# A fp32 trunk on one core: seven products for chunk 7 of a fast group, later transposes, and alternating first groups

## The chip, the core and the metric

The kernel runs on one core of a Trainium2 chip. The engines are TensorE (PE in the profile, with its weight loads as PEld), VectorE (DVE), ScalarE (ACT), GpSimd (POOL) and SyncE (SP), which issues most DMAs. The metric is the device time of one execution in microseconds, as the median of several runs.

## The reference

Two decoder layers on x of 256 x 2048 in fp32. Layer 0 is a recurrent block (RG-LRU) and a SwiGLU FFN; then one K/V projection; layer 1 is sliding-window attention with sinks and a second SwiGLU FFN.

```python
def swiglu_ffn(x, g, w_in, w_out):
    h = rms_norm(x, g)
    gate, up = jnp.split(h @ w_in, 2, axis=-1)
    return x + (jax.nn.silu(gate) * up) @ w_out

def recurrent_block(x, g, w_in, conv_w, conv_b, w_rg, b_rg, w_ig, b_ig, lam, w_out):
    h = rms_norm(x, g)
    y_branch, x_branch = jnp.split(h @ w_in, 2, axis=-1)
    xb = causal_depthwise_conv(x_branch, conv_w, conv_b)
    hs = rg_lru(xb, w_rg, b_rg, w_ig, b_ig, lam)
    return x + (hs * jax.nn.gelu(y_branch)) @ w_out
...
    for layer in range(DEPTH):
        if layer < N_REC:
            x = recurrent_block(...)
        else:
            if layer == N_REC:
                k_band, v_band = shared_kv(x, kv_norm_g, w_kv, k_norm_g)
            x = attn_block(...)
        x = swiglu_ffn(x, norm2_g[layer], ffn_w_in[layer], ffn_w_out[layer])
```

D_MODEL is 2048 and D_FF 5632, so an FFN has w_in of 2048 x 11264 and w_out of 5632 x 2048.

## The kernel before

**Products in three parts.** Each fp32 operand is split in a high part (rounded to the format that the matmul reads) and a low part (the rest); a product is high x high + high x low + low x high. So a 128x128 block of weights costs three matmuls over 256 columns (the 256 tokens).

**Jobs.** The work is a list of 704 jobs, each with a weight tile of 512 KB (128 x 1024). `stream` (L381) goes through them: at job i it issues the load of job i+4 on SP into one of 4 raw tiles (`load`, L334), splits the weights of job i+3 into one of 4 pairs of hi and lo tiles (`split`, L351: ACT copies hi at L359, DVE subtracts lo at L360), and then issues the matmuls of job i. Other work (norms, gates, recombinations) is written as generators that are advanced between jobs by budgets of DVE and ACT time; a scheduler then orders the rows on each engine, so the order is to be read from the built program.

**Groups.** A group is 8 jobs (chunks, 0 to 7) over the 2048 input features that fill 4 banks of PSUM; two sets of 4 banks take turns. `group` (L411) issues 24 matmuls of 128x256 a chunk at L407. A chunk named in its `sync` has three pairs of them (both columns of a bank half) as one matmul of 128x512 instead, 21 instructions for the same work; the two banks that hold these need another copy and addition at the end.

**FFN.** w_in has 22 groups of 8 chunks, w_out 4 groups of 22 chunks. In w_in the groups 4, 6, ..., 20 are fast (`FAST`). In a fast group, the chunks named in `PAIRS` (0, 1, 2, 4, 5, 6) multiply 2x2 blocks by seven products (the Strassen-Winograd scheme) in place of eight: 21 matmuls at L565 in place of 24. They need combined activations, made once per FFN in `normed` (a tile mx[p] for every chunk of `PAIRS`; four operations on 128x128 blocks, a copy and a subtraction), and combined weights, made for each chunk in `mix` (L362): DVE adds and subtracts raw blocks (L371, L372, L373), ACT copies the high parts (L370 of the plain blocks, L374 of the combined ones), and DVE subtracts the low parts (L375, L376). Chunks 3 and 7 are plain, 24 matmuls at L565. In chunks 0 and 4 the products of combined weights come first, in the others last. At a fast group's end `joined` recombines the products on ACT and DVE, and appends four transposes on PE (L761, `turn`) to a list that `flush` empties: at chunk 4 of the next fast group, or for the last one at chunk `pre` of the end group, group 21. The groups between the fast ones, and the end group, are plain groups of 192 narrow matmuls each (L407); the end group has `sync` chunks 0, 3, 4 and 5. After it, `ffn_out` runs by `project`, whose chunks 0, 1, 2 have wide matmuls.

**LRU.** Its groups run in the order x0 x1 x2 g0 x3 g1 y0 ..., the first two being the first 16 jobs. The background task `first` (in `run`) prepares the 16 slices of x (a scaled copy on ACT, a subtraction on DVE, `gained`), then squares them for the norm (tiles sq), and the norm's matmuls (L516, L518) follow. x comes in four tiles of 512 KB; the first is loaded with job 0, the others by SP behind the loads of jobs 1, 2 and 3.

Of the kernel before, what the change touches and what calls it, by code (L numbers as in the profile page):

```python
# [21 lines left out]
ND = D // P  # L22
NH = DFF // P
# [26 lines left out]
class Trunk:  # L50
# [2 lines left out]

    ORDER = "x0 x1 x2 g0 x3 g1 y0 g2 g3 y1 g4 g5 y2 g6 g7 y3"
    NORM0 = 11
    NORM = 6
    MISC = 4

# [3 lines left out]
    SYNC = (0, 1, 2)  # L62
    PLAIN = 4
    FAST = tuple(range(4, 21, 2))
    PAIRS = (0, 1, 2, 4, 5, 6)
    EVEN = (0, 4)
    OWED = 9000.0
    BUSY = 780.0
# [7 lines left out]
    def __init__(self, ctx, tc, dram):  # L76
        self.tc, self.nc, self.d = tc, tc.nc, dram
        nc = self.nc
        const = ctx.enter_context(tc.tile_pool(name="const", bufs=1))
        psum = ctx.enter_context(tc.tile_pool(name="psum", bufs=1, space=bass.MemoryType.PSUM))  # L80
        self.par = const.tile([P, NPAR], F32, name="par")
        self.con = const.tile([P, NCON], F32, name="con")
        self.cc = const.tile([P, 32], F32, name="cc")
        self.rstd = [const.tile([P, T + 2], F32, name=f"rstd{i}") for i in range(2)]
        self.nm, self.nt = (const.tile([P, T + 2], F32, name=n) for n in ("nm", "nt"))
        self.r2 = const.tile([P, 2], F32, name="r2")
        self.rrs = [const.tile([P, 48], F32, name=f"rr{i}") for i in range(2)]
        self.zero = const.tile([P, P + T], F32R, name="zero")
        const.tile([P, PAD], F32, name="pad")
        self.raw = [const.tile([P, 1024], F32, name=f"raw{i}") for i in range(4)]  # L90
        self.hi = [const.tile([P, 1024], F32R, name=f"hi{i}") for i in range(4)]
        self.lo = [const.tile([P, 1024], F32R, name=f"lo{i}") for i in range(4)]
        self.tmps = deque(const.tile([P, T], F32, name=f"t{i}") for i in range(4))
        self.halves = deque(const.tile([P, T], F32, name=f"h{i}") for i in range(4))
        self.sq = deque(const.tile([P, T], F32, name=f"sq{i}") for i in range(3))
        self.acc = self.sq.popleft()
        self.whole = [deque((i, 0) for i in range(self.NEAR, self.WORK)), deque((i, 0) for i in range(self.NEAR))]
        self.stamp = 0
        self.tick = -2 * self.LD
        self.keep = False  # L100
        self.part = {(d, n): deque() for d in (F32, F32R) for n in (False, True)}
        self.spool = const
        for i in range(self.WORK):
            if i == self.NEAR:
                const.tile([P, 16], F32, name="step")
            const.tile([P, 4 * T], F32, tag=f"s{i}", name=f"s{i}")
        self.held = {}
        self.x, self.xt = [None] * 4, [None] * 4
        for i in range(4):
            self.place(i)  # L110
        self.dram = ctx.enter_context(tc.tile_pool(name="dram", bufs=1, space=bass.MemoryType.DRAM))
        self.away = {}
        self.sets = [[psum.tile([P, 512], F32, name=f"b{4 * i + j}") for j in range(4)] for i in range(2)]
        self.banks = deque(b for q in self.sets for b in q)
        self.misc = 0
        self.started = False
        self.jobs = []
        self.mixed = {}
        self.pend = deque()
        self.bg = deque()  # L120
        self.dve = 0.0
        self.act = 0.0
# [211 lines left out]
    def load(self, i):  # L334
        dma = self.nc.sync.dma_start
        raw, src = self.raw[i % 4], self.jobs[i][0]
        if i == 0:

            self.nc.scalar.dma_start(self.x[0][:, 0:2, :], self.d["x"][:, 0:2, :])
            self.nc.scalar.dma_start(self.par, self.d["par"])  # L340
            for h in range(2):
                dma(raw[:, 512 * h:512 * h + 512], src[:, 512 * h:512 * h + 512])
            dma(self.x[0][:, 2:4, :], self.d["x"][:, 2:4, :])
        else:
            dma(raw, src)
            if i < 4:
                dma(self.x[i], self.d["x"][:, 4 * i:4 * i + 4, :])
        if i == 4:
            dma(self.con, self.d["con"])

# [156 lines left out]

    def norm(self, r, wait=NORM):

# [48 lines left out]
    def fast_group(self, src, xn, mx, g, done, final):  # L558
# [49 lines left out]
        for c in range(8):  # L608
            def mm(hi, lo, c=c):
                if c == 0:  # L610
                    st["ps"] = self.bank4()
                if c == self.EVEN[1]:
                    self.flush()
                (fast if c in self.PAIRS else plain)(c, hi, lo)
                if c == 7:
                    done(st["ps"])
            self.jobs.append((src(c), mm, (c in self.PAIRS) + (c in self.EVEN)))

# [5 lines left out]
    def ffn(self, l, xs, r, gains, rn, col, out=None):  # L624
# [3 lines left out]
        xn = [Val() for _ in range(ND)]  # L628
# [64 lines left out]
        for g in range(NH // 2):  # L693
# [77 lines left out]
            src = lambda c, g=g: w[g, c]  # L771
            if g < self.PLAIN:
                self.group(src, ND, xs, start, g == self.PLAIN - 1, self.SYNC, four=True)
            elif g in self.FAST:
                self.fast_group(src, xn, mx, g, joined, g == self.FAST[-1])
            else:
                end = g == self.FAST[-1] + 1
                self.group(src, ND, xn, direct, g == NH // 2 - 1, (0, 3, 4, 5) if end else (), True, 3 if end else None)
            if g == 0:
                def begin():  # L780
                    self.spawn(normed())
# [4 lines left out]
        n = len(self.jobs)  # L786
# [57 lines left out]
    def lru(self, gains, rn):  # L844
# [149 lines left out]

        for step in self.ORDER.split():
            {"x": x_group, "y": y_group, "g": gates}[step[0]](int(step[1]))
        self.project(self.d["lru_out"], ND, zs, gains, rn)


# [307 lines left out]
    def run(self):  # L1307
        nc, d = self.nc, self.d
        self.rv = {i: Val() for i in range(4)}
        self.rstd = {0: self.rstd[0], 1: self.rstd[1], 2: self.rstd[0], 3: self.rstd[1]}  # L1310
        vals = lambda: [Val() for _ in range(ND)]
        self.xs0, x1, xk, x2, x3 = (vals() for _ in range(5))

        def first():
            for k in range(ND):
                self.gained(k, [(C_N1A, self.xs0)])
                yield 2 * (k == 1)
            for k in range(ND):
                yield from self.squares(k)
            yield from self.norm(0, self.NORM0)  # L1320
            self.decay()
        self.spawn(first())
        nc.vector.memset(self.zero[:, :].bitcast(F32), 0.0)
        p = self.bank()
        for _ in range(self.WARM):
            nc.tensor.matmul(p[:, 0:T], self.zero[:, 0:P], self.zero[:, P:P + T], start=True, stop=True)
        self.free_bank(p)

        self.lru([(C_N2A, x1)], 1)
        self.ffn(0, x1, 1, [(C_KVG, xk)], 2, C_N2A)  # L1330
        self.kv(xk, 2, [(C_N1B, x2)])
        self.attn(x2, 2, [(C_N2B, x3)], 3)
        self.ffn(1, x3, 3, None, None, C_N2B, d["out"])
        self.stream()
# [64 lines left out]
```

## Time and profile before

| | before |
|---|---|
| median of 3 runs | 1977.0 us (1976.61 to 1977.29) |
| the profiled execution | 1976.85 us, span 1975.1 us, clock 1.000 |
| PE busy | 1966.8 us, 16548 matmuls |
| DVE busy | 1514.6 us (77%) |
| ACT busy | 1131.8 us (57%) |
| L565, seven-product chunks and plain chunks of fast groups | 1224 + 1296 + 612 matmuls |
| DMA | 384.96 MB, mean 195 GB/s |

All rows are of one execution. "L407" is a line of the kernel; a row of a timeline is start, length, engine, line, operation, written tile, read tiles, and in brackets the idle time ahead with what ended it. A matmul's recorded length holds its way through the array; the distance from start to start is what it costs.

### The profile page before, as it was taken

Reading aid. Unit: us, or ns where it says so; the run is one execution under the profiler, and the core shown is the slowest. Engines: PE = TensorE matmul, PEld = TensorE weight load, DVE = VectorE, ACT = ScalarE, POOL = GpSimd, SP = SyncE. Lnnn points to the kernel's source line nnn. Section 1 sums busy time; section 2 is a strip of 40 time slices with the busy share of each in tenths; the row PEclk is TensorE's granted clock in tenths of the full one; section 3 lists DMA queues with packets and bytes.
Section 4 is the critical chain, followed back from the end, with each engine's and each line's share of the span. In section 5 each row is a group of like instructions: output and inputs, shape, how many; then the busy total and the mean of one; then the engine's idle time right before and its main releaser. Section 6 shows DMA issues by size and latency. Waiting matters only on the chain. (4 is left out here: it accounts for less than half of the span.)

```text
span 1975.1 us, 40195 instructions
## 1 busy us (share of the span) xinstructions
PE 1966.8 (100%) x16548; PEld 1925.4 (97%) x16548; DVE 1514.6 (77%) x2399; ACT 1131.8 (57%) x1656; POOL 0.2 (0%) x4
## 2 busy tenths in 40 slices
PE   9999999999999999999999999999999999999999
PEld 9999999999999999999998789999999999999999
DVE  8989868998888887554667776698889888954443
ACT  7788756555555566444556675565555555744442
POOL 0000000000000000000000000000000000000000
PEclk9999999999999999999999999999999999999999
DMA  7555665566555566556554335656555666666663
GB/s 272 191 191 178 216 217 192 186 206 208 202 199 197 200 218 224 194 190 201 194 182 145 122 118 171 213 186 206 191 199 200 203 207 202 235 203 203 203 204 128
DMA packets 107320, 384.96 MB, mean 195 GB/s; under 512 B 11904, under 2 KB 14080, under 8 KB 107136
## 3 DMA queue, kind: packets, MB, share of 16 engines
q1 hardware_dynamic: 106848, 381.99, 57.7%
q8 instruction: 129, 2.11, 0.4%
q14 instruction: 55, 0.45, 0.1%
q10 hardware_dynamic: 288, 0.40, 0.1%
HBM read 376.06 MB, written 6.29 MB: 194 GB/s over the span
## 5 line engine op out<-in xcount | busy, mean ns | idle before, releaser
L407 PE MATMUL b<-s,hi 128*128 128x256 f32 (+1 forms) x7934 | 1060.1, 281 | 1.6 <-ACT s L133 1.2
L407 PEld LDWEIGHTS b<-s,hi 128*128 128x128 f32 x7934 | 986.5, 188 | 14.7 <-ACT s L133 2.2
L360 DVE TENSOR_TENSOR lo<-raw,hi 128x1024 fp32r<-128x1024 f32 (+1 forms) x597 | 726.9, 1222 | 354.8 <-ACT hi L359 351.9
L359 ACT ACTIVATE hi<-raw 128x1024 fp32r<-128x1024 f32 (+1 forms) x597 | 628.3, 1056 | 502.3 <-PE b L407 400.9
L407 PE MATMUL b<-s,lo 128*128 128x256 f32 x4096 | 607.3, 277 | 0.0
L407 PEld LDWEIGHTS b<-s,lo 128*128 128x128 f32 x4096 | 530.4, 188 | 0.2
L374 ACT ACTIVATE s<-s 128x1024 fp32r<-128x1024 f32 x108 | 114.8, 1063 | 183.6 <-DVE s L373 183.6
L565 PE MATMUL b<-hi,s 128*128 128x256 f32 x1224 | 203.2, 277 | 0.0
L565 PEld LDWEIGHTS b<-hi,s 128*128 128x128 f32 x1224 | 174.1, 188 | 0.0
L565 PE MATMUL b<-s,s 128*128 128x256 f32 x1296 | 168.4, 279 | 0.0
L565 PEld LDWEIGHTS b<-s,s 128*128 128x128 f32 x1296 | 157.2, 189 | 0.0
L376 DVE TENSOR_TENSOR s<-s,s 128x1024 fp32r<-128x1024 f32 x108 | 132.0, 1223 | 23.6 <-ACT s L374 23.6
L565 PE MATMUL b<-lo,s 128*128 128x256 f32 x612 | 145.8, 277 | 0.0
L565 PEld LDWEIGHTS b<-lo,s 128*128 128x128 f32 x612 | 104.2, 188 | 0.0
L133 ACT ACTIVATE s<-s 128x512 fp32r<-128x512 f32 (+3 forms) x174 | 86.1, 523 | 30.4 <-DVE s L142 18.5
L370 ACT ACTIVATE hi<-raw 128x768 fp32r<-128x768 f32 x108 | 88.0, 839 | 24.2 <-issue 14.0
L375 DVE TENSOR_TENSOR lo<-raw,hi 128x768 fp32r<-128x768 f32 x108 | 101.5, 953 | 0.0
L371 DVE TENSOR_TENSOR s<-raw 128x512 f32<-128x512 f32 x108 | 74.3, 688 | 22.0 <-DMA raw<-in_ffn_in 21.6
L1289 PE MATMUL b<-hi,s 128*128 128x512 f32 x256 | 83.5, 407 | 0.0
L142 DVE TENSOR_TENSOR s<-s,s 128x512 fp32r<-128x512 f32 (+2 forms) x141 | 74.9, 559 | 4.7 <-ACT s L133 4.7
L133 ACT ACTIVATE s<-b 128x256 fp32r<-128x256 f32 (+4 forms) x134 | 58.8, 468 | 24.9 <-PE b L1263 6.8
L142 DVE TENSOR_TENSOR s<-b,s 128x512 f32<-128x512 f32 (+3 forms) x126 | 63.4, 533 | 5.3 <-ACT s L133 3.9
(115 smaller groups left out, 1101.0 us busy)
## 6 DMA issues: line engine op xcount, KB each, us to landing
raw<-in_ffn_in SPq DMA_DIRECT2D x352, 512.0 KB, 3.5
raw<-in_ffn_out SPq DMA_DIRECT2D x176, 512.0 KB, 3.4
raw<-in_lru_in SPq DMA_DIRECT2D x63, 512.0 KB, 3.8
raw<-in_lru_out SPq DMA_DIRECT2D x32, 512.0 KB, 4.1
raw<-in_w_q SPq DMA_DIRECT2D x32, 512.0 KB, 3.3
raw<-in_w_o SPq DMA_DIRECT2D x32, 512.0 KB, 3.5
raw<-in_gate SPq DMA_DIRECT2D x8, 512.0 KB, 3.9
away<-s SPq DMA_DIRECT2D x8, 512.0 KB, 3.6
```

Of the source, the lines that this page charges most:

```text
L133: self.nc.scalar.activation(out, in_, func, **kw)
L142: self.nc.vector.tensor_tensor(out, a, b, op)
L359: self.nc.scalar.activation(hi[:, q], raw[:, q], AF.Copy)
L360: self.nc.vector.tensor_tensor(lo[:, q], raw[:, q], hi[:, q].bitcast(F32), ALU.subtract)
L370: act(hi[:, q], raw[:, q], AF.Copy)
L371: tt(two(d[:, 0:2 * T]), two(raw[:, T:3 * T]), raw[:, 0:T].unsqueeze(1).to_broadcast([P, 2, T]), ALU.subtract)
L374: act(mh[:, :], d[:, :], AF.Copy)
L375: tt(lo[:, q], raw[:, q], hi[:, q].bitcast(F32), ALU.subtract)
L376: self.mark = tt(ml[:, :], d[:, :], mh[:, :].bitcast(F32), ALU.subtract)
L407: self.nc.tensor.matmul(ps[f][:, 0:c1 - c0], w, x2[k][:, c0:c1], start=f not in begun, stop=last and all(q[1] != f for q in todo[n + 1:]))
L565: nc.tensor.matmul(st["ps"][b][:, h % 2 * T:(h % 2 + n) * T], x, w, start=b not in st["begun"], stop=True, skip_group_check=True)
L1289: nc.tensor.matmul(st[g][b][:, :], x, q, start=c + kt == 0 and x is xh and q is wh, stop=c == 7 and kt == 1 and q is wl)
```

## The change

Three edits. Chunk 7 joins `PAIRS`, so that seven of eight chunks of a fast group go by seven products, and `normed` makes one more combined tile. The end group loses its wide matmuls, and its `flush` goes from chunk 3 to chunk 6. The first 16 jobs are put in another order: x0 and x1 alternate for six chunks (x0 c0, x1 c0, x0 c1, x1 c1, x0 c2, x1 c2), then the rest of x0 and the rest of x1; the x tiles 1, 2, 3 are loaded behind jobs 2, 5 and 7, and `first` waits until the tile it needs has been issued. Lines of the changed kernel are 2 to 4 higher up to L381, and 4 higher in the groups (L407 becomes L411, L565 L569, L761 L765, L376 L380).

```diff
--- before.py
+++ after.py
@@ -53,6 +53,7 @@
 
     ORDER = "x0 x1 x2 g0 x3 g1 y0 g2 g3 y1 g4 g5 y2 g6 g7 y3"
     NORM0 = 11
+    XLOAD = {2: 1, 5: 2, 7: 3}
     NORM = 6
     MISC = 4
 
@@ -62,7 +63,7 @@
     SYNC = (0, 1, 2)
     PLAIN = 4
     FAST = tuple(range(4, 21, 2))
-    PAIRS = (0, 1, 2, 4, 5, 6)
+    PAIRS = (0, 1, 2, 4, 5, 6, 7)
     EVEN = (0, 4)
     OWED = 9000.0
     BUSY = 780.0
@@ -110,6 +111,7 @@
             self.place(i)
         self.dram = ctx.enter_context(tc.tile_pool(name="dram", bufs=1, space=bass.MemoryType.DRAM))
         self.away = {}
+        self.got = 0
         self.sets = [[psum.tile([P, 512], F32, name=f"b{4 * i + j}") for j in range(4)] for i in range(2)]
         self.banks = deque(b for q in self.sets for b in q)
         self.misc = 0
@@ -343,8 +345,10 @@
             dma(self.x[0][:, 2:4, :], self.d["x"][:, 2:4, :])
         else:
             dma(raw, src)
-            if i < 4:
-                dma(self.x[i], self.d["x"][:, 4 * i:4 * i + 4, :])
+            if i in self.XLOAD:
+                n = self.XLOAD[i]
+                dma(self.x[n], self.d["x"][:, 4 * n:4 * n + 4, :])
+                self.got = n
         if i == 4:
             dma(self.con, self.d["con"])
 
@@ -775,7 +779,7 @@
                 self.fast_group(src, xn, mx, g, joined, g == self.FAST[-1])
             else:
                 end = g == self.FAST[-1] + 1
-                self.group(src, ND, xn, direct, g == NH // 2 - 1, (0, 3, 4, 5) if end else (), True, 3 if end else None)
+                self.group(src, ND, xn, direct, g == NH // 2 - 1, (), True, 6 if end else None)
             if g == 0:
                 def begin():
                     self.spawn(normed())
@@ -994,6 +998,8 @@
 
         for step in self.ORDER.split():
             {"x": x_group, "y": y_group, "g": gates}[step[0]](int(step[1]))
+        first = [8 * (i % 2) + i // 2 for i in range(6)]
+        self.jobs[:16] = [self.jobs[i] for i in first + [i for i in range(16) if i not in first]]
         self.project(self.d["lru_out"], ND, zs, gains, rn)
 
 
@@ -1313,6 +1319,8 @@
 
         def first():
             for k in range(ND):
+                while self.got < k // 4:
+                    yield 1
                 self.gained(k, [(C_N1A, self.xs0)])
                 yield 2 * (k == 1)
             for k in range(ND):
```

What stands on DVE where the last chunks of a fast group of FFN 0 are split, before (L371 to L376 are a mix, raw2 that of chunk 6; L360 is a plain split, the last two rows being chunk 7 and the next group's chunk 0):

```order
L376 TENSOR_TENSOR s2_5204<-s3_5202,s1_5203 128x1024
L375 TENSOR_TENSOR lo0_81<-raw0_73,hi0_77 128x768
L375 TENSOR_TENSOR lo1_82<-raw1_74,hi1_78 128x768
L371 TENSOR_TENSOR s5_5234<-raw2_75 128x512
L372 TENSOR_TENSOR s5_5234<-raw2_75,s5_5234 128x256
L375 TENSOR_TENSOR lo2_83<-raw2_75,hi2_79 128x768
L373 TENSOR_TENSOR s5_5234<-raw2_75,s5_5234 128x256
L376 TENSOR_TENSOR s3_5236<-s5_5234,s0_5235 128x1024
L360 TENSOR_TENSOR lo3_84<-raw3_76,hi3_80 128x1024
L360 TENSOR_TENSOR lo0_81<-raw0_73,hi0_77 128x1024
```

and now (lines 4 higher, raw2 chunk 6, raw3 chunk 7):

```order
L380 TENSOR_TENSOR s2_5216<-s5_5214,s4_5215 128x1024
L375 TENSOR_TENSOR s1_5246<-raw2_75 128x512
L379 TENSOR_TENSOR lo2_83<-raw2_75,hi2_79 128x768
L376 TENSOR_TENSOR s1_5246<-raw2_75,s1_5246 128x256
L375 TENSOR_TENSOR s3_5281<-raw3_76 128x512
L377 TENSOR_TENSOR s1_5246<-raw2_75,s1_5246 128x256
L376 TENSOR_TENSOR s3_5281<-raw3_76,s3_5281 128x256
L377 TENSOR_TENSOR s3_5281<-raw3_76,s3_5281 128x256
L380 TENSOR_TENSOR s5_5248<-s1_5246,s6_5247 128x1024
L379 TENSOR_TENSOR lo3_84<-raw3_76,hi3_80 128x768
L380 TENSOR_TENSOR s1_5283<-s3_5281,s0_5282 128x1024
L364 TENSOR_TENSOR lo0_81<-raw0_73,hi0_77 128x1024
```

The three additions of chunk 7 (on s3) now stand ahead of the last subtraction of chunk 6 (s5), and two subtractions of chunk 7 where one was.

On PE around the transposes of the last fast group in FFN 1's end group, before (hi3 and lo3 are the end group's chunk 3; b is a bank, s a tile of activations):

```order
L407 MATMUL b5_145<-s18_14431,lo2_83 128x256
L407 MATMUL b6_146<-s18_14431,lo2_83 128x256
L407 MATMUL b7_147<-s18_14431,lo2_83 128x256
L761 MATMUL b0_140<-con_62,s21_19098 128x128 x4
L407 MATMUL b6_146<-s9_14498,hi3_80 128x256
L407 MATMUL b4_144<-s9_14498,hi3_80 128x512 x2
L407 MATMUL b5_145<-s9_14498,hi3_80 128x512
L407 MATMUL b6_146<-s9_14498,hi3_80 128x256
```

and now:

```order
L411 MATMUL b5_145<-s19_14648,lo1_82 128x256
L411 MATMUL b6_146<-s19_14648,lo1_82 128x256
L411 MATMUL b7_147<-s19_14648,lo1_82 128x256
L765 MATMUL b0_140<-con_62,s27_19213 128x128 x4
L411 MATMUL b4_144<-s26_14747,hi2_79 128x256 x2
L411 MATMUL b5_145<-s26_14747,hi2_79 128x256 x2
L411 MATMUL b6_146<-s26_14747,hi2_79 128x256 x2
```

The transposes stand ahead of chunk 6 (hi2) instead of chunk 3, and the 128x512 matmuls behind them are gone.

SP's queue at the start, before (raw is a weight tile, s33 to s36 the tiles of x, con the constants):

```order
L342 DMA raw0_73<-in_lru_in 128x512 x2
L343 DMA s36_134<-in_x 128x512
L345 DMA raw1_74<-in_lru_in 128x1024
L347 DMA s35_135<-in_x 128x1024
L345 DMA raw2_75<-in_lru_in 128x1024
L347 DMA s34_136<-in_x 128x1024
L345 DMA raw3_76<-in_lru_in 128x1024
L347 DMA s33_137<-in_x 128x1024
L345 DMA raw0_73<-in_lru_in 128x1024
```

and now:

```order
L344 DMA raw0_73<-in_lru_in 128x512 x2
L345 DMA s36_134<-in_x 128x512
L347 DMA raw1_74<-in_lru_in 128x1024
L347 DMA raw2_75<-in_lru_in 128x1024
L350 DMA s35_135<-in_x 128x1024
L347 DMA raw3_76<-in_lru_in 128x1024
L347 DMA raw0_73<-in_lru_in 128x1024
L353 DMA con_62<-in_con 128x1026
L347 DMA raw1_74<-in_lru_in 128x1024
L350 DMA s34_136<-in_x 128x1024
```

The tiles s35, s34 and s33 moved behind the loads of jobs 2, 5 and 7.

## The prediction

> **What bounds the kernel now.** I read the page's busy rows first.
>
> ```profile
> span 1975.1 us, 40195 instructions
> PE 1966.8 (100%) x16548; PEld 1925.4 (97%) x16548; DVE 1514.6 (77%) x2399; ACT 1131.8 (57%) x1656; POOL 0.2 (0%) x4
> ```
>
> TensorE (PE) is busy for all but 8.3 us, so time can only come from fewer matmuls, a faster pace, or those 8.3 us. VectorE (DVE) is the next engine. The chain of waits says the same for the stretch the change touches, a pair of one fast and one plain group:
>
> ```profile
> 1395.25 9.96 PE b L565 x87
> 1405.20 0.44 PE b L761 x4
> 1405.64 9.96 PE b L565 x87
> 1415.60 21.76 PE b L407 x192
> ```
>
> 87 matmuls of a half fast group take 9.96 us (114.5 ns each); 192 of a plain group take 21.76 us (113.3 ns each). Nothing but PE stands in the chain there: DVE and ScalarE (ACT) keep ahead, and the question is whether they still do with the new work. The windows view gives the load in one such pair, among the heaviest on DVE:
>
> ```profile
> 1489.40:1531.50 42.10, 42.10 (x373) 42.10 (x372) 37.38 (x50) 23.15 (x28) 0.00 (x0) 1.00 0.60 208
> ```
>
> The columns are length, then PE, weight loads, DVE, ACT, POOL, granted clock, DMA share, GB/s. DVE has 4.7 us free of 42.1, ACT 19; the clock is full.
>
> **The change part by part.** *Chunk 7 by seven products.* The timeline of PE at the end of the last fast group shows a mixed chunk (6), a plain one (7), and the plain group behind them:
>
> ```profile
> 1705.10 0.39 PE L565 MATMUL b<-hi,s 128*128 128x256 f32 x2
> 1706.12 1.52 PE L565 MATMUL b<-s,s 128*128 128x256 f32 x12
> 1707.48 0.62 PE L565 MATMUL b<-hi,s 128*128 128x256 f32 x4
> 1710.20 1.98 PE L407 MATMUL b<-s,hi 128*128 128x512 f32 x13
> ```
>
> Chunk 6, 21 matmuls, runs from 1705.10 to 1707.48: 2.38 us. Chunk 7, 24 matmuls, runs to 1710.20: 2.72 us. The saving is 0.34 us a group, for 9 fast groups in each of 2 FFNs 18 x 0.34 = **-6.1 us** (the same as 54 matmuls x 113.3 ns). The end of a mixed chunk (twelve matmuls from mixed weights at 1706.12) does not slow what follows: the 24 behind it keep 113.3 ns.
>
> The Trainium skill ("TensorE: Matmul & The Clock Gate", section "Back-to-back issue gap") gives N/2.4 + 2.5 ns for an isolated warm matmul, 109.2 ns at 256 columns, and says that in a real stream of weight loads and matmuls both set the spacing. By the formula 54 matmuls would be an estimated 5.9 us; the row's 113.3 ns decides.
>
> What it costs elsewhere: chunk 7's weights are no longer split by one subtraction (L360) but mixed.
>
> ```profile
> L360 DVE TENSOR_TENSOR lo<-raw,hi 128x1024 fp32r<-128x1024 f32 x595 | 725.5, 1223 | 351.1 <-ACT hi L359 348.2
> L371 DVE TENSOR_TENSOR s<-raw 128x512 f32<-128x512 f32 x108 | 74.3, 688 | 22.0 <-DMA raw<-in_ffn_in 21.6
> L372 DVE TENSOR_TENSOR s<-raw,s 128x256 f32<-128x256 f32 x108 | 45.7, 423 | 2.3
> L373 DVE TENSOR_TENSOR s<-raw,s 128x256 f32<-128x256 f32 x108 | 45.7, 423 | 2.3
> L375 DVE TENSOR_TENSOR lo<-raw,hi 128x768 fp32r<-128x768 f32 x108 | 101.5, 953 | 0.0
> L376 DVE TENSOR_TENSOR s<-s,s 128x1024 fp32r<-128x1024 f32 x108 | 132.0, 1223 | 23.6 <-ACT s L374 23.6
> L374 ACT ACTIVATE s<-s 128x1024 fp32r<-128x1024 f32 x108 | 114.8, 1063 | 183.6 <-DVE s L373 183.6
> L370 ACT ACTIVATE hi<-raw 128x768 fp32r<-128x768 f32 x108 | 88.0, 839 | 24.2 <-issue 14.0 <-ACT hi L359 4.8 <-ACT hi L370 2.5
> ```
>
> On DVE 0.688 + 0.423 + 0.423 + 0.953 + 1.223 = 3.71 us in place of 1.22: 2.5 us more per fast group. The heaviest pair goes from 37.4 to at most 39.9 us of a new 41.8 (42.1 - 0.34): 95% busy, still under PE. ACT gets L370 and L374 (1.90 us) in place of one copy of about a microsecond, with 19 us free. Cost on the path nothing, as long as each mix is done in time, which is a matter of latency and not of load:
>
> ```profile
> 1701.04 1.22 DVE L376 TENSOR_TENSOR s<-s,s 128x1024 fp32r<-128x1024 f32 x1 [1.12 <-ACT s L374]
> 399.27 1.23 DVE L376 TENSOR_TENSOR s<-s,s 128x1024 fp32r<-128x1024 f32 x1 [0.46 <-ACT s L374]
> 400.42 4.62 DVE L360 TENSOR_TENSOR lo<-raw,hi 128x1024 fp32r<-128x1024 f32 x4
> 403.45 0.62 PE L565 MATMUL b<-hi,s 128*128 128x256 f32 x4
> ```
>
> In the steady state (first row) chunk 6's last mix ends at 1702.26 and is read from 1706.12 on: 3.9 us early. DVE waits 1.12 us for L374 just there, and in the new order the L371 to L373 of chunk 7 stand in that hole. Back to back, an instruction starts a little before the last one's recorded end (400.42 behind 399.27: 1.15 apart for 1.23), so L371 to L373 take some 1.3 us against 1.12; then L375 (0.87) and L376 (1.15). Chunk 7's mix ends at about 1704.5, and is read 1.02 us into the chunk (1706.12 - 1705.10), at 1708.50: **4 us early**; up to four short instructions of other work ahead of it leave 1.5 to 4.
>
> The first fast group of an FFN is tightest, for its mixes follow the catch-up on the norm. Its chunk 6 mix starts at 399.27 behind a hole of 0.46 only. The new three add 1.3 - 0.5 = 0.8 us, then 0.87 and two of 1.15: done at about 403.3, read at 403.45 + 1.02 = 404.47: about **1.1 us early**. I take 0; were the estimate wrong by more than that, the stall is the second rival's. The new tiles of the norm (four short operations of 128x128, a copy, a subtraction: below 2 us of DVE per FFN) fall into holes of the group before:
>
> ```profile
> 370.38 1.23 DVE L360 TENSOR_TENSOR lo<-raw,hi 128x1024 fp32r<-128x1024 f32 x1 [1.34 <-ACT hi L359]
> 373.08 0.69 DVE L371 TENSOR_TENSOR s<-raw 128x512 f32<-128x512 f32 x1 [1.47 <-DMA raw<-in_ffn_in]
> ```
>
> Those hold 2.8 us; if they did not cover it, it would come off the 1.1 us. No DMA is added in the FFNs and the weights' loads keep their order on SP's queue; they are gated by the buffers' release, which the shorter chunk makes earlier by 0.34 us.
>
> *The end group.* Its four chunks with wide matmuls become narrow ones. Ahead of the transposes and behind them stand:
>
> ```profile
> 1715.65 1.98 PE L407 MATMUL b<-s,hi 128*128 128x256 f32 x16
> 1717.46 1.07 PE L407 MATMUL b<-s,lo 128*128 128x256 f32 x8
> 1718.37 0.60 PE L761 MATMUL b<-con,s 128*128 128x128 f32 x4
> 1718.73 2.07 PE L407 MATMUL b<-s,hi 128*128 128x256 f32 x13
> 1720.63 1.07 PE L407 MATMUL b<-s,lo 128*128 128x256 f32 x8
> 1716.87 0.69 DVE L142 TENSOR_TENSOR s<-s 128x512 f32<-128x512 f32 x1
> ```
>
> Wide matmuls buy no time as such: 13 instructions with three wide ones stand for the 16 of 1715.65. But behind the transposes the 16 take 1.90 us (1718.73 to 1720.63) instead of 1.81, which is 118.8 ns each, until the wide ones end it. Moved to the seventh chunk without wide ones, chunks 6 and 7 run at that pace: 48 x (117.5 to 118.8 - 113.3) = 0.20 to 0.26 us, less the 0.09 paid now, about +0.13 an FFN, **+0.3** in all. ffn_out's first chunk has wide matmuls again, which bounds it. What the move avoids: the recombined tile (row 1716.87) is done at 1717.56, 0.8 us ahead of the transposes. With 2.5 us more of mixing ahead of it on DVE the old place would have stalled PE by 1.7 us; at the new place, three chunks or 8.2 us later, it cannot. The transposed tile is read by chunk 20 of ffn_out's 22, some 50 us on, and its splitting starts only after the end group, so nobody waits for the later transposes.
>
> *The start.* x0 and x1 alternate for six chunks, so a pair of prepared x tiles is needed every second chunk:
>
> ```profile
> 15.91 2.05 PE L407 MATMUL b<-s,hi 128*128 128x256 f32 x16
> 17.79 1.10 PE L407 MATMUL b<-s,lo 128*128 128x256 f32 x8
> 18.86 2.15 PE L407 MATMUL b<-s,hi 128*128 128x256 f32 x16
> 22.21 2.15 PE L407 MATMUL b<-s,hi 128*128 128x256 f32 x16 [0.25 <-ACT hi L359]
> 25.14 2.05 PE L407 MATMUL b<-s,hi 128*128 128x256 f32 x16
> 20.79 0.42 ACT L133 ACTIVATE sq<-s 128x256 f32<-128x256 f32 x1 [1.04 <-DVE sq L142]
> ```
>
> At the undisturbed pace here (16 in 1.88 us, 117.5 ns) a chunk is 2.82 us. From 15.91 to 25.14 three chunks take 9.23 us instead of 8.46: 0.77 us of waits for weights that ACT copies late, since it is held by the preparation of x. Spreading that over twice the chunks removes between 0 and 0.77; most of it, I take **-0.6**. The x tiles' DMAs go behind loads 2, 5 and 7 instead of 1, 2 and 3 on SP, so weights land earlier and x tiles 2 and 3 later, each still some chunks ahead of its first use. No matmul is added, and both groups are done at the same job as before.
>
> Sum: -6.1 + 0.3 - 0.6 = **-6.4 us** on the profiled execution's 1976.85, 1970.4. That execution lies 0.15 under the median 1977.0, so the median should be **1970.6 us**.
>
> **The rivals.** *One: DVE late for chunk 7 in every fast group (slower).* The place is L376 of chunk 7. For it: DVE would be 95% busy, and it takes its rows in order, so one L376 that waits for ACT holds the subtractions queued behind it. The Trainium skill (same page, section "Architectural detail") says that ACT and DVE queues are strict FIFO; the trace agrees with rows such as 1701.04, where DVE stands idle for 1.12 us with work queued behind. Against it: 1.5 to 4 us of lead. It decides once that lead is gone. Then PE stalls, and behind a stall it runs at 117.5 ns (row 15.91) until wide matmuls, of which a plain group has none: 192 x 4.2 ns = 0.81 us and a stall of 0.3 us or more, 18 times, +20 on 1970.6: **1990 us**. A bare change of pace behind the longer mixed stretch, without stall, is 18 x 0.81 = +14.6: **1985**. Against that: the 24 at full pace behind chunk 6.
>
> *Two: only the first fast group of each FFN is late.* The lead of 1.1 us is the thinnest. A stall of 0.5 us and the pace of 0.81 us, twice: +2.6, **1973.2 us**.
>
> *Three: the LRU part shifts.* The start's new order moves every row of ACT and DVE up to the gates. One wait there is as long as:
>
> ```profile
> 155.82 0.42 ACT L133 ACTIVATE s<-h 128x256 f32<-128x256 f32 x1 [3.28 <-DVE h L142]
> 159.03 2.54 PE L407 MATMUL b<-s,hi 128*128 128x256 f32 x16 [0.76 <-ACT s L133]
> ```
>
> PE stalls 0.76 us there and then keeps the slow pace until the next wide matmul. If the start gains nothing and one more stall of this size with its slow stretch comes (0.76 + some 250 x 4.2 ns = 1.8), it is +2.4: **1973.0**. It may also vanish: 1968.8.
>
> **How the numbers follow.** Forecast 0.72, rival one 0.08 (its two forms together), rival two 0.10, rival three 0.10 (two thirds of it upwards). The forecast's own range is 1969.3 to 1972.0 (start 0 to -0.77, pace 0 to +0.5, small shifts). The range takes in rivals two and three: down to 1968.5 (the third's gain with all of the 0.77), up to 1974.2 (the second with stalls of 1 us); rival one is left out. What a measurement can tell from no change is 0.2%, 3.95 us: 1973.05 and 1980.95 are the bounds. Below lie the forecast and more than half of rivals two and three: 0.84. Above 1980.95 lies rival one, 0.08; between, 0.08.
>
> **What would show it.** Right: a chain of waits in which the second half of a fast group is 84 matmuls in some 9.6 us and no other engine stands between; PE's matmuls 54 fewer, less the 24 wide ones that become two each (16518 in all); DVE at 39 to 40 us in a pair of 41.8; plain groups still at 21.76 us; 0.77 us less between 15.9 and 25.1. Wrong: a plain group at 22.6 us (pace), idle time of PE on L376's tile (rival one), the same in the first fast group alone (rival two), or gaps before 200 us that were not there (rival three).

## The result, and the profile after

The changed kernel takes 1969.75 us as the median of 7 executions (1969.5 to 1972.61), against 1977.0 us of the kernel before, also 7: ratio 0.9966, interval 0.9955 to 0.9978. That is 7.25 us less; 6.4 were forecast (1970.6). Seven more executions later (in the experiments) had a median of 1970.94 (1968.56 to 1971.89), so all 14 have a median of 1970.2 and spread over 4 us, where the 28 of the kernel before beside them spread over 1.9 (1976.13 to 1978.04).

The profiled execution of the changed kernel took 1970.22 us, 6.63 less than the profiled one before. From its page:

```profile
span 1968.4 us, 40256 instructions
PE 1960.3 (100%) x16518; PEld 1920.3 (98%) x16518; DVE 1541.0 (78%) x2477; ACT 1144.2 (58%) x1672; POOL 0.2 (0%) x4
```

PE still fills the span; it lost 6.5 us and 30 instructions (54 fewer, and 24 wide ones became two each). Its chain of waits, for one pair of a fast and a plain group:

```profile
1474.91 9.96 PE b L569 x87
1484.87 0.44 PE b L765 x4
1485.31 9.62 PE b L569 x84
1494.92 21.76 PE b L411 x192
```

The half group with chunk 7 is 84 matmuls in 9.62 us instead of 87 in 9.96, and the plain group behind it keeps 21.76. The same pair in the windows view (columns as before):

```profile
1484.87:1526.65 41.78, 41.78 (x369) 41.78 (x368) 38.76 (x54) 23.96 (x28) 0.00 (x0) 1.00 0.64 209
```

DVE is at 38.8 of 41.8 us in this pair, the heaviest of FFN 1 (the heaviest of FFN 0 has 39.0), and PE has no gap. Set beside each other chunk by chunk, the two profiles differ by these amounts in the end (a minus is time won):

| stretch | forecast | measured |
|---|---|---|
| first matmul of a chunk at 7.65 us instead of 7.42 | - | +0.23 |
| the first 16 chunks from there | -0.6 | -0.76 |
| the rest of the LRU part and FFN 0's first groups | 0 | -0.12 |
| 18 chunks 7 | -6.1 | 18 x -0.34 = -6.1 |
| end group of FFN 0 / first chunks of its ffn_out | +0.13 | +0.09 / +0.19 |
| end group of FFN 1 | +0.13 | -0.02 |
| attention part | 0 | -0.10 |

### The profile page after: what moved, and what is told of

It reads as the page before. It is cut to its first block, busy times and chain, and to the rows that moved or that the text cites. A ratio compares the mean times of both kernels' runs of the same rounds, so it can differ in the third digit from the quotient of the medians.

```text
span 1968.4 us, 40256 instructions
## 1 busy us (share of the span) xinstructions
PE 1960.3 (100%) x16518; PEld 1920.3 (98%) x16518; DVE 1541.0 (78%) x2477; ACT 1144.2 (58%) x1672; POOL 0.2 (0%) x4
## 5 line engine op out<-in xcount | busy, mean ns | idle before, releaser
L411 PE MATMUL b<-s,hi 128*128 128x256 f32 (+1 forms) x7958 | 1060.0, 280 | 1.4 <-ACT s L135 1.2
L411 PEld LDWEIGHTS b<-s,hi 128*128 128x128 f32 x7958 | 987.5, 188 | 13.2 <-ACT s L135 2.1
L364 DVE TENSOR_TENSOR lo<-raw,hi 128x1024 fp32r<-128x1024 f32 (+1 forms) x579 | 702.6, 1220 | 320.2 <-ACT hi L363 312.7
L363 ACT ACTIVATE hi<-raw 128x1024 fp32r<-128x1024 f32 (+1 forms) x579 | 608.1, 1056 | 469.8 <-PE b L411 405.4
L411 PE MATMUL b<-s,lo 128*128 128x256 f32 x4096 | 607.0, 276 | 0.0
L411 PEld LDWEIGHTS b<-s,lo 128*128 128x128 f32 x4096 | 530.3, 188 | 0.2
L378 ACT ACTIVATE s<-s 128x1024 fp32r<-128x1024 f32 x126 | 131.8, 1058 | 189.1 <-DVE s L377 189.0
L569 PE MATMUL b<-s,s 128*128 128x256 f32 x1512 | 195.9, 279 | 0.0
L569 PEld LDWEIGHTS b<-s,s 128*128 128x128 f32 x1512 | 183.0, 189 | 0.0
L569 PE MATMUL b<-hi,s 128*128 128x256 f32 x1044 | 178.0, 277 | 0.0
L380 DVE TENSOR_TENSOR s<-s,s 128x1024 fp32r<-128x1024 f32 x126 | 153.7, 1220 | 6.0 <-ACT s L378 5.9
L569 PEld LDWEIGHTS b<-hi,s 128*128 128x128 f32 x1044 | 152.3, 188 | 0.0
L569 PE MATMUL b<-lo,s 128*128 128x256 f32 x522 | 132.5, 276 | 0.0
L379 DVE TENSOR_TENSOR lo<-raw,hi 128x768 fp32r<-128x768 f32 x126 | 118.6, 952 | 0.0
L374 ACT ACTIVATE hi<-raw 128x768 fp32r<-128x768 f32 x126 | 102.1, 832 | 9.1 <-ACT s L378 4.9
L569 PEld LDWEIGHTS b<-lo,s 128*128 128x128 f32 x522 | 92.7, 188 | 0.0
```

The lines of the kernel that those rows point to most:

```text
L363: self.nc.scalar.activation(hi[:, q], raw[:, q], AF.Copy)
L364: self.nc.vector.tensor_tensor(lo[:, q], raw[:, q], hi[:, q].bitcast(F32), ALU.subtract)
L374: act(hi[:, q], raw[:, q], AF.Copy)
L378: act(mh[:, :], d[:, :], AF.Copy)
L379: tt(lo[:, q], raw[:, q], hi[:, q].bitcast(F32), ALU.subtract)
L380: self.mark = tt(ml[:, :], d[:, :], mh[:, :].bitcast(F32), ALU.subtract)
```

## The experiments

### The parts apart

**Chunk 7 alone.**

```diff
-    PAIRS = (0, 1, 2, 4, 5, 6)
+    PAIRS = (0, 1, 2, 4, 5, 6, 7)
```

> Only the seventh mixed chunk (PAIRS with 7); the end group and the start stay as before. Theory (edits add up, the move of the transposes is needed): 18 fast-group halves of 9.62 us instead of 9.96, -6.1 us, and PE stalls at the old place of the transposes (chunk 3 of the end group), since in the changed kernel the recombined tile was done 2.1 us after that chunk's start: +2 us an FFN and some 0.1 of pace, so 1977.0 - 6.1 + 4.2 = 1975.1 us. Rival (the move was not needed, DVE catches up): no idle PE ahead of the transposes, 1970.9 us.

Measured: 1979.37 us in the median of 10 (1976.7 to 1981.48), before 1976.9; ratio 1.0011 (1.0001 to 1.0020). The profiled execution is the lowest, 1976.7. Each of the 18 chunks 7 won its 0.34 us, and the old place of the transposes gave back 1.91 us in FFN 0 and 2.35 us in FFN 1. On PE in FFN 1:

```profile
1717.90 0.66 PE L761 MATMUL b<-con,s 128*128 128x128 f32 x4 [1.94 <-DVE s L142]
```

The transposes wait 1.94 us for the recombined tile: 1.7 from the rows of before were forecast. So without the move of the transposes most of the gain would be gone. The rest of the gap to the expected 1975.1 is not in this part: this profile also has stalls in the second fast group of FFN 1 (0.45 us in chunk 3, 0.61 us in chunk 6) and a slow stretch of 0.6 us in the LRU part, and the median lies 2.7 us above it. What the other executions lost was not profiled, but the mean clock that was granted to each of them is known, and by and large it falls as the time rises: 1.000 in the three from 1976.7 to 1978.48, 0.999 in the three from 1978.51 to 1979.72, 0.998 in the four from 1979.67 to 1981.48. In a profile below (the mix two subtractions late), a stretch of 3.41 us at half the clock follows a long wait of PE; it costs 1.7 us and lowers the mean clock by 0.0009. None, one or two such stretches in an execution, behind the transposes' waits, would fit these numbers; that this is what happened is not shown.

**The start alone.** The job order, the x loads behind jobs 2, 5 and 7, and the wait in `first`; nothing else.

> Only the alternating first groups with their later x loads. Theory: the 0.77 us of waits between 15.9 and 25.1 us vanish and nothing after 60 us changes: between -0.8 and -0.5 us, 1976.3 us. Rival (the LRU part shifts): the stall of 0.92 us at 158 us grows or vanishes, 1975 or 1978.

Measured: 1975.67 us (10 executions, 1973.89 to 1977.95), before 1976.9; ratio 0.9994 (0.9985 to 1.0004), so the executions alone do not show a gain. In the profile the first 16 chunks won 0.76 us, as in the changed kernel. The profiled execution was the slowest one all the same, since it lost 0.60 in the LRU part and 1.25 us in FFN 0's end group. On PE there:

```profile
752.24 0.66 PE L765 MATMUL b<-con,s 128*128 128x128 f32 x4 [1.03 <-DVE s L144]
```

The transposes at the old place stalled even without the new mixes: the margin that the profile of before showed there (0.8 us in both FFNs) is not safe from one execution to the next. Moving them is worth something by itself.

**The end group alone.**

```diff
-                self.group(src, ND, xn, direct, g == NH // 2 - 1, (0, 3, 4, 5) if end else (), True, 3 if end else None)
+                self.group(src, ND, xn, direct, g == NH // 2 - 1, (), True, 6 if end else None)
```

> Only the end group without wide matmuls and with the transposes ahead of chunk 6. Theory by the prediction: +0.13 us an FFN, since chunks 6 and 7 run at 117.6 ns until the next wide matmul: 1977.3 us. Rival, from the changed kernel's trace (slow until the third chunk of ffn_out in FFN 0, slow for 16 matmuls only in FFN 1): the slow pace ends neither by wide matmuls nor always without; then the two FFNs differ again, in whichever way, by 0.1 to 0.3 us.

Measured: 1977.21 us (10 executions, 1976.54 to 1977.71), before 1976.9; ratio 1.0002 (0.9992 to 1.0011). By the profile +0.28 us in FFN 0 and 0 in FFN 1, as in the changed kernel. So the rival holds in this profile: the sum of +0.3 was right, its split and its reason were not. The executions alone do not tell +0.3 us from nothing.

**Chunk 7 and the end group, the start as before.**

```diff
-    PAIRS = (0, 1, 2, 4, 5, 6)
+    PAIRS = (0, 1, 2, 4, 5, 6, 7)
-    ..., (0, 3, 4, 5) if end else (), True, 3 if end else None)
+    ..., (), True, 6 if end else None)
```

> The seventh mixed chunk and the new end group, the start as before. Theory (edits add up: the start is worth its 0.77 us and no more): 0.8 us above the changed kernel, 1971 us, with the same leads of the mixes in the first fast groups on average. Rival (the start also sets how the weight loads stand to PE later, and with it how often the first fast groups stall): stalls in more of the first fast groups than in the two profiles of the changed kernel, 1973 us or more.

Measured: 1972.01 us (10 executions, 1970.47 to 1972.31), before 1976.91; ratio 0.9975 (0.9965 to 0.9984). That is 1.8 us above the median of the changed kernel's 14, where the start accounts for 0.77. Its profile, the fastest execution, shows no stall in a fast group. Whether the other 1 us is stalls in the unprofiled executions stays open; the two medians were not taken side by side, and the kernels spread by 2 and 4 us.

### The wide matmuls and the slow pace

```diff
-    ..., (), True, 6 if end else None)
+    ..., (0, 6) if end else (), True, 6 if end else None)
```

> The changed kernel with wide matmuls in chunks 0 and 6 of the end group, that is, right behind the transposes. Theory of the prediction (wide matmuls end the slow pace): 0.13 to 0.2 us less an FFN, 1969.4 us, and chunk 7 of both end groups at 2.72 us. Rival (they don't decide): FFN 0's end group and ffn_out's first chunks are as slow as before, 1969.8 us.

Measured: 1970.91 us (8 executions, 1969.5 to 1973.88), before 1976.99; ratio 0.9972 (0.9961 to 0.9982). In the changed kernel, PE in FFN 0 behind the transposes:

```profile
755.66 0.60 PE L765 MATMUL b<-con,s 128*128 128x128 f32 x4
756.01 2.13 PE L411 MATMUL b<-s,hi 128*128 128x256 f32 x16
757.98 1.10 PE L411 MATMUL b<-s,lo 128*128 128x256 f32 x8
...
761.75 2.03 PE L411 MATMUL b<-s,hi 128*128 128x512 f32 x13
763.62 1.10 PE L411 MATMUL b<-s,lo 128*128 128x256 f32 x8
764.56 2.04 PE L411 MATMUL b<-s,hi 128*128 128x256 f32 x13
766.44 1.10 PE L411 MATMUL b<-s,lo 128*128 128x256 f32 x8
767.38 2.00 PE L411 MATMUL b<-s,hi 128*128 128x256 f32 x13
```

With wide matmuls directly behind them:

```profile
756.72 0.60 PE L765 MATMUL b<-con,s 128*128 128x128 f32 x4
757.07 2.11 PE L411 MATMUL b<-s,hi 128*128 128x256 f32 x13
759.02 1.10 PE L411 MATMUL b<-s,lo 128*128 128x256 f32 x8
...
762.79 2.03 PE L411 MATMUL b<-s,hi 128*128 128x512 f32 x13
764.65 1.10 PE L411 MATMUL b<-s,lo 128*128 128x256 f32 x8
765.60 2.04 PE L411 MATMUL b<-s,hi 128*128 128x256 f32 x13
```

In both, the eight matmuls on low parts take 0.94 to 0.95 us (763.62 to 764.56 and 766.44 to 767.38; 764.65 to 765.60), 117.5 to 119 ns each, in chunks with wide ones and without, and only the third chunk of ffn_out goes back to 113.3. In FFN 1 the same code of the changed kernel is back after 16 narrow ones (chunk 6 in 2.81 us, chunk 7 in 2.72), with no wide one in sight. So **wide matmuls do not end the slow pace** as the prediction had it. This pattern came out the same in ten of the eleven profiles with the transposes at chunk 6, so it is hardly chance; in the other one (all eight chunks by seven products) FFN 0 too is back after 16 matmuls. Nor is it the FFN alone: with the transposes at chunk 3 and late (chunk 7 alone), it is FFN 0 that is back after one chunk and FFN 1 that needs three. What ends the slow pace is open. The time of 1970.91 decides nothing here: the profiled execution (1972.40) also had a stall of 0.25 us in the first fast group, with a slow plain group behind it, and two of 0.17 and 0.63 us in the second fast group of FFN 1.

### The lead of the mixes

**The changed kernel again**, for another profile.

> The changed kernel once more, for a second profile. Theory: every stage within 0.1 us of the first profile, 1969.8 us. Rival (the pace after the transposes is left to chance, which would also explain why its runs lay between 1969.5 and 1972.6): FFN 0's end group takes another time than before, or a plain group runs at 22.6 us.

Measured: 1970.94 us (7 executions, 1968.56 to 1971.89), before 1976.9; ratio 0.9967 (0.9956 to 0.9979). The profiled execution took 1971.89, 1.67 more than the first. It has two disturbances in the first fast groups. In the first profile, DVE and PE at chunk 7 of FFN 0's first one:

```profile
402.28 1.23 DVE L380 TENSOR_TENSOR s<-s,s 128x1024 fp32r<-128x1024 f32 x1
```

```profile
403.81 1.52 PE L569 MATMUL b<-s,s 128*128 128x256 f32 x12
405.17 1.07 PE L411 MATMUL b<-s,hi 128*128 128x256 f32 x8
```

The mix ends at 403.51; its low part is read by the third of the twelve, at 404.04: 0.53 us early. That margin is the lead of the mix. In the second profile:

```profile
402.18 1.23 DVE L380 TENSOR_TENSOR s<-s,s 128x1024 fp32r<-128x1024 f32 x1
```

```profile
403.27 1.64 PE L569 MATMUL b<-s,s 128*128 128x256 f32 x12
404.74 2.04 PE L411 MATMUL b<-s,hi 128*128 128x256 f32 x16
406.62 1.10 PE L411 MATMUL b<-s,lo 128*128 128x256 f32 x8
```

DVE comes 0.1 us earlier but PE 0.54 (in this execution the first chunk had started 1.0 us earlier, of which 0.55 were left here). The lead is down to 0.1 us, the twelve take 1.47 us instead of 1.36, and the plain group behind runs at 117.5 ns: 0.85 us more. In FFN 1 the second fast group stalled. On PE, then in the chain of waits:

```profile
1407.83 1.91 PE L569 MATMUL b<-s,s 128*128 128x256 f32 x12
```

```profile
1407.01 1.24 DVE s L380
1408.24 0.04 issue
1408.29 3.92 PE b L569 x31
1412.21 22.61 PE b L411 x192
```

Here DVE stands in the chain: the mix of chunk 6 ends at 1408.24, 0.2 us after it was wanted; 0.39 us of stall, and then the plain group takes 22.61 us instead of 21.76. The next half group is normal. So rival two is real, in some executions and in the first two fast groups, and in the second of them through chunk 6.

**The mix of chunk 7 later by one and by two subtractions.**

```diff
-        self.mark = tt(ml[:, :], d[:, :], mh[:, :].bitcast(F32), ALU.subtract)
+        for _ in range(2 if self.jobs[i][2] == 3 else 1):
+            self.mark = tt(ml[:, :], d[:, :], mh[:, :].bitcast(F32), ALU.subtract)
```

The mark 3 is that of chunk 7; the second kernel has `range(3 ...`.

> The changed kernel, with the last subtraction of chunk 7's mix (L380) done twice in a row, the second over the first: its result is 1.15 us later, nothing else differs. Leads of that mix in the profile of the changed kernel: 0.53 us in the first fast group of each FFN, 1.1 to 1.6 in the next five or so, 3.3 to 3.8 later. Theory: two stalls of 0.6 us, and 0.8 us of slow pace behind each: +2.8 us, 1972.6 us; the other groups hold. Rival (the lead is not what decides): within 0.5 us of the changed kernel.

Measured: 1981.3 us (10 executions, 1974.83 to 1984.58), before 1976.99; ratio 1.0019 (1.0008 to 1.0029). On PE and DVE in the first fast group:

```profile
406.87 1.42 PE L570 MATMUL b<-s,s 128*128 128x256 f32 x10 [2.12 <-DVE s L381]
```

```profile
404.46 1.22 DVE L364 TENSOR_TENSOR lo<-raw,hi 128x1024 fp32r<-128x1024 f32 x1
405.59 1.22 DVE L381 TENSOR_TENSOR s<-s,s 128x1024 fp32r<-128x1024 f32 x1
```

Here another subtraction got in between, so that the result was 2.3 us late and PE stalled for 2.1. Ten of 18 chunks 7 stalled (0.1 to 2.4 us), not two: in FFN 1, four leads that were 2.4 to 3.8 had shrunk below zero. The stalls make up 9.1 of the 10.0 us between the two profiled executions; no plain group behind them was slow. So the extra 1.15 us is not simply taken off one lead: DVE's order changed with it, and its later work came later too.

> The same subtraction three times in a row: 2.3 us later. Theory: 1.8 us late in the first fast groups, 0.7 to 1.2 us late in the groups with a lead of 1.1 to 1.6, and DVE's load (38.7 + 2.3 = 41.0 of 41.4 us) leaves the others no room to keep their leads; a stall of about 1 us and 0.8 us of slow pace in each of 18 groups: +20 to +30 us, 1990 to 2000 us. Rival (a stall is not followed by slow pace, and later groups keep their lead): 9 or 10 stalls of 1 us, 1979 us.

Measured: 2004.84 us (4 executions, 2003.38 to 2008.41), before 1976.99; ratio 1.0143 (1.0128 to 1.0158), so +35 us over the changed kernel, above what was expected. From its chain of waits, plain groups in FFN 1:

```profile
1390.68 24.14 PE b L412 x192
...
1434.84 21.76 PE b L412 x192
...
1478.20 22.61 PE b L412 x192
```

Sixteen of the 18 chunks 7 stalled; together that is 27.6 us, and 7.3 us more lie in six plain groups. So the price of rival one is real. But the slow pace followed only about a third of the stalls: six of sixteen, some 0.8 us each. Two of these six took longer still, the first row by another 1.5 us, though PE has no gap in them. A window behind that stall shows why (the third number from the end is the granted clock):

```profile
1391.00:1394.00 3.00, 3.00 (x16) 3.00 (x15) 2.93 (x6) 0.00 (x0) 0.00 (x0) 0.50 0.79 221
```

Around it, 16 matmuls (from 1390.52 on) take 3.35 us instead of 1.81. In this profile the clock is at 0.50 for 3.41 us behind the two longest waits of PE (4.08 and 3.65 us, in the first fast group of each FFN) and at 1.00 everywhere else. Each such stretch costs 1.7 us, 3.4 of the 35 in all. It is not the slow pace of 117.6 ns, which comes at a clock of 1.00.

**Chunk 3 by seven products as well.**

```diff
-    PAIRS = (0, 1, 2, 4, 5, 6, 7)
+    PAIRS = tuple(range(8))
```

With no plain chunk nothing writes the first half of bank 0, which the recombination still adds, so this term is computed from stale data; the amount of work is as told.

> The changed kernel with chunk 3 by seven products as well: all eight, 54 matmuls fewer again, 18 mixes more. DVE busy in a pair was 37.4 us before and 38.7 us with seven (heaviest pair), so about 40.0 of 41.4 us with eight. Theory (latency, not load, decides): the first fast group of each FFN, whose chunk 7 mix was only 0.5 us early, stalls by 1 to 3 us, the others hold: 1969.8 - 6.1 + 2 to 6 = 1966 to 1970 us. Rival (DVE is the bound): every fast group stalls and runs on at 117.6 ns, 16 x 0.8 us or more on top: 1980 us or more.

Measured: 2035.78 us (4 executions), before 1976.99; ratio 1.0298 (1.0283 to 1.0314): 66 us slower than the changed kernel with 54 matmuls less. By the groups of its PE and by a window of FFN 1:

```profile
L569 PE MATMUL b<-s,s 128*128 128x256 f32 x1728 | 250.4, 288 | 35.1 <-ACT s L378 22.3 <-DVE s L380 11.6
```

```profile
1470.00:1520.00 50.00, 47.49 (x399) 46.57 (x399) 44.60 (x64) 25.87 (x31) 0.00 (x0) 1.00 0.57 190
```

PE stood 35 us waiting for mixes, while DVE was 89% busy. That is half of the loss: PE is also busy for 1992.0 us, 31.7 more than in the changed kernel with fewer matmuls, of which 8.5 us are five stretches of 3.41 us at half the clock; the rest was not taken apart. So neither expectation fits: every group stalls, far beyond two, but DVE is not full. The chain that ended last runs through all engines (PE 25%, DVE 7%, DMA 3%, ACT 2% of the span, against PE 40% and the others 0% in the changed kernel), so they seem to wait for each other in turns.

### Ways to a longer lead

**Chunk 7 plain again in the first fast group, and in the first two.**

```diff
+        pairs = self.PAIRS[:-1] if g in (4,) else self.PAIRS
```

The second kernel has `(4, 6)`.

> The changed kernel, but chunk 7 of the first fast group of each FFN (group 4) is plain again: 6 matmuls more, +0.68 us. Theory (the stalls behind the 2 to 3 us between its executions come from the mixes of the first two fast groups; without chunk 7's in group 4 the backlog of DVE is 2.2 us less there and in group 6): no stall in group 4 and 6 in the profile, executions within 1 to 1.5 us of each other, median 1970.5 us. Rival (the spread comes from elsewhere): executions spread by 3 us or more, median 1971.5 us.

Measured: 1970.97 us (6 executions, 1970.65 to 1971.32), before 1976.91; ratio 0.9969 (0.9957 to 0.9981). The spread is 0.7 us, the smallest of all with the new chunk 7, though in six executions only. No stall in groups 4 and 6 in the profile, as the theory said, but one in group 8, where chunk 6's mix was 0.4 us late. On PE there:

```profile
485.29 1.40 PE L570 MATMUL b<-s,s 128*128 128x256 f32 x10 [0.32 <-DVE s L380]
```

> The same for groups 4 and 6 of each FFN: 12 matmuls more than the changed kernel, +1.36 us. Theory: no stall in the first fast groups at all, 1971 us, executions within 1 us. Rival: as spread as the changed kernel, 1972 us.

Measured: 1971.42 us (7 executions, 1970.21 to 1972.43), before 1976.91; ratio 0.9971 (0.9960 to 0.9982). The theory falls: the spread is 2.2 us. In the profile chunk 6 of the first fast group, with its mix 0.1 us early, slowed PE and the plain group behind was 0.85 us longer, though chunk 7 there was plain. What chunk 7 adds is a thinner lead, not the only one that is thin.

**Five raw weight tiles.**

```diff
-    LD = 4
+    LD = 5
-    WORK = 37
+    WORK = 36
-    self.raw[i % 4]
+    self.raw[i % 5]
```

> The changed kernel with five raw weight tiles instead of four, each load issued five jobs ahead, and one working tile less (36) to make room; nothing else. In its profiles DVE waits 2.5 to 3.0 us at 370 us for a weight tile to land, just ahead of the first fast group, and 43.5 us in all on that line. Theory (the thin lead in the first fast groups comes from these waits, since a late load shifts DVE's whole chain while PE goes on): the wait at 370 goes, chunk 7's mix in the first fast groups is 1.5 us or more early instead of 0.1 to 0.5, no stall in fast groups, 1969.5 us and executions within 1.5 us. Rival (the planner's order or the hi and lo tiles, still four, set the lead, or the missing tile stalls other work): leads as before, spread of 3 us, 1970 us or more.

Measured: 1971.99 us (11 executions, 1969.76 to 1974.3), before 1976.58; ratio 0.9979 (0.9970 to 0.9988): no better than the changed kernel. DVE's waits for weight tiles, in the changed kernel and then here:

```profile
DVE s L375 <- DMA raw<-in_ffn_in: 43.5, 38, 2.8
```

```profile
DVE s L375 <- DMA raw<-in_ffn_in: 15.3, 18, 1.8
```

They are down to a third, and chunk 7's lead was 2.3 to 5.0 us from the second fast group on (1.1 to 3.8 in the changed kernel), in the first ones 1.2 and 0.55. So the loads did set the lead, in part. But the order on DVE changed too, and stalls came up elsewhere. PE and DVE at chunk 3 of group 6 in FFN 1:

```profile
1400.28 0.50 PE L569 MATMUL b<-lo,s 128*128 128x256 f32 x2 [1.06 <-DVE lo L364]
```

```profile
1397.87 1.22 DVE L380 TENSOR_TENSOR s<-s,s 128x1024 fp32r<-128x1024 f32 x1
1399.00 1.22 DVE L364 TENSOR_TENSOR lo<-raw,hi 128x1024 fp32r<-128x1024 f32 x1
```

The plain chunk's subtraction now stands behind a mix of a chunk that is needed later, and PE waits 1.06 us for it. Not DVE's order alone: ACT's copy of the same weights, which the subtraction needs, is done at 1398.44 only, since ACT had waited 5.14 us for the additions of a mix (L377 on DVE) and did that mix and another first. It was the place in both queues. (The Trainium skill has ACT's and DVE's queues as strict FIFO, "TensorE: Matmul & The Clock Gate", section "Architectural detail"; these rows agree.) Both sides were right in half: the lead grew, and the order on DVE and ACT took it back.

None of the variants has a lower median than the changed kernel.

## Why the prediction was right or wrong

**Right: the matmuls.** 18 x 0.34 us came out to the hundredth: 2.38 us for each chunk 7 that was not held up, in every profile with the edit. The formula of the Trainium skill ("TensorE: Matmul & The Clock Gate", "Back-to-back issue gap": 109.2 ns at 256 columns, an estimated 5.9 us) would have been a little low; the row's 113.3 ns held.

**Right: the transposes had to move.** Without the move they cost 1.91 and 2.35 us (chunk 7 alone).

**Right in size: the start.** 0.76 us of waits vanished, 0.6 had been taken from a bound of 0.77. The chunks now follow at 2.83 us:

```profile
16.13 2.05 PE L411 MATMUL b<-s,hi 128*128 128x256 f32 x16
18.96 2.04 PE L411 MATMUL b<-s,hi 128*128 128x256 f32 x16
21.79 2.05 PE L411 MATMUL b<-s,hi 128*128 128x256 f32 x16
24.61 2.05 PE L411 MATMUL b<-s,hi 128*128 128x256 f32 x16
```

When the first chunk starts was not in the sum; it moved between 6.5 and 7.7 us in these profiles, and most of that came back as shorter or longer waits behind it.

**Mis-sized: DVE's load and the leads.** The load was put too high and the leads too long. The pair at 37.4 us of DVE was put at 39.9 at most and measured 38.8 (it was not the heaviest: the first pair of each FFN had 38.3 before). The lead of chunk 7 in the first fast groups was put at 1.1 us, counted to the first of the twelve matmuls, which is 1.4 to the third, the one that reads the low part. To the third it measured 0.53 in the first profile, 0.1 and 0.27 in the second; the later groups, put at 1.5 to 4, measured 1.1 to 3.8.

The step behind this is that the new operations of the norm were to fall into holes on DVE ahead of the group, one of them a wait of 1.47 us for a weight tile. That wait grew instead. In the first and in the second profile:

```profile
373.46 0.69 DVE L375 TENSOR_TENSOR s<-raw 128x512 f32<-128x512 f32 x1 [2.50 <-DMA raw<-in_ffn_in]
```

```profile
373.40 0.69 DVE L375 TENSOR_TENSOR s<-raw 128x512 f32<-128x512 f32 x1 [2.99 <-DMA raw<-in_ffn_in]
```

The load that DVE waits for is itself issued right behind one of DVE's subtractions, the one that frees the tile (369.04 and 369.07 us before, 369.68 and 369.70 in the first profile). Measured from PE's start of the group, that was 1.3 us later than before, so the hole moved and was not filled; in the second profile the load also took 4.2 us instead of 3.7. The mix of chunk 7 is not what does it: with chunk 7 plain in the first group the wait was 2.92 us. With five tiles it was 1.46 us again. Nor does PE's own place decide: chunk 7 alone began this group 1.4 us later than the changed kernel (386.99 us against 385.62) and had a lead of only 0.21 there.

The prediction also worked out chunk 7's lead only and left chunk 6's where it was. But chunk 7's three additions stand ahead of chunk 6's last subtraction, and chunk 6's lead went from 1.7 to 4.1 us before to 0.7 to 3.5 in the first profile. In the kernels without a delayed mix, the stalls in the second and third fast groups are chunk 6's (0.39 us in the second profile, 0.61 with chunk 7 alone, 0.59 with chunk 7 plain in the first group) or the plain chunk 3's (0.45 us with chunk 7 alone), not chunk 7's. So rival two, given one chance in ten, happens in some executions of this kernel rather than in all or none, and in more places than were looked at.

**Wrong reason: the end group.** "Until wide matmuls end it" was wrong. The +0.3 us came out (+0.27) because FFN 0 paid twice what was said and FFN 1 nothing; that the two halves of the error cancel is luck.

**Half right: the pace behind a stall.** The price of 0.81 us for a slow plain group measured 0.85, but it does not follow each stall (6 of 16 with the mix two subtractions late, none of ten with it one late), and it can follow a mix that is in time by 0.1 us. What the prediction had no term for is the clock: two long waits were followed by 3.41 us at half the clock, 1.7 us each.

**Rival three** showed only as noise: single stretches of the LRU part differed by 0.6 to 0.8 us either way between executions. For instance the slow stretch behind the stall at 158 us, the same 0.76 in the first profile as before, was missing in the second, which had a stall of 0.69 at 187 us instead.

## What to carry to other kernels

When work is moved onto an engine that is 90% busy, the sum of its load says little: read how long before its first use each result is done, in the tightest place, and ask what moves producer and consumer apart from one execution to the next; a second profile of the same kernel is the cheapest way to see it. An edit that makes one result later should be looked at together with everything that was just in time before (here the transposes and chunk 6's mix), since that is where the gain is given back. A hole in which an engine waits for a load is free only if the load does not itself wait for what you put in front of it.

## What the runs showed of the hardware that was not expected

- PE has two paces for the same stream of 128x256 matmuls at full granted clock, 113.3 and 117.6 ns. A stall or transposes can put it into the slower one, for some chunks (0.1 to 0.8 us in all) or for a whole plain group (0.85 us). Matmuls of 128x512 do not reliably bring it back, and with the transposes at chunk 6 the same code behaves one way in FFN 0 and another in FFN 1, the same in ten of eleven profiles. What decides is open.
- A result can be in time and still cost something. In these profiles the three mixes that were 0.08 to 0.11 us early made their chunk 0.09 to 0.12 us longer; the seven that were 0.17 to 0.23 us early cost nothing.
- Behind a wait of PE of 3.65 or 4.08 us the granted clock went to 0.50 for 3.41 us. With all eight chunks by seven products it did so five times, behind shorter waits too (one of 2.36 us), and another wait of 2.36 us was not followed by it. What decides was not looked into.
- Making one DVE result 1.15 us later cost 11 us, 2.3 us later 35 us (1970.2 to 1981.3 and 2004.84), though DVE and PE had room on paper: past the lead, most chunks 7 wait (9.1 and 27.6 us in all in the two profiles).
- Kernels whose mixes are barely in time spread by 0.7 to 10 us between executions (1974.83 to 1984.58 with the mix one subtraction late, at clocks of 0.999 and 1.000), the kernel before by 1.9.
